# A two-layer decoder trunk: the first two weight blocks by halves of the channels, held weight splits, dummy products before the second mixer, and r·k on VectorE

## The chip, the cores and the metric

The kernel runs on one core of one Trainium2 chip. The metric is device time of one execution in microseconds (us); the time before is the median of three runs, 1817.96 us (1816.81 to 1820.01).

## The reference, cut to what matters

Two decoder layers work on 256 rows of 1024 channels, in float32:

```
h = rmsnorm(x, mix_norm_g); u = h @ w_in
y_rw  = rwkv7_time_mix(token_shift(u[rw columns]), ...)   # needs sum(r*k*r_k) per head
y_nsa = nsa_mix(u[nsa columns], ...)
x = x + concat(y_rw, y_nsa) @ w_out
x = x + cross_attention(rmsnorm(x, cross_norm_g), rmsnorm(mem, mem_norm_g), wq, wkv, wo)
x = x + (swiglu(rmsnorm(x)) in layer 0, top-2-of-8 experts in layer 1)
```

Each layer so has three places where a norm of `x` is followed by a product of all 256 rows with a large weight matrix: the mixer's input projection, the cross-attention's query projection and the channel mixer's first matrix.

## The kernel before, in words

**Three products for one.** A float32 weight block of [128 x 8 x 128] goes into two float32r parts by `split` (L382, L383): `wh`, a copy on ScalarE, and `wl = w - wh`, a subtraction on VectorE. The rows are split likewise into `hh` and `hl`. Each product of a channel group k is then three matmuls, `wh·hh`, `wh·hl` and `wl·hh` (L405 to L407), with 256 columns each. `proj_b` (L396) does this for weight blocks of 256 outputs: per block it takes one PSUM bank (tag `pj`), splits half b = 0, issues its 24 matmuls over the eight groups k, then half b = 1, and calls `evac` when both are done. The 48 matmuls of a block are one unit of work below.

**The start of a stage.** `parts_t` (L434) turns the rows: for each pair of channel groups k2 it issues four 128x128 transposes into one PSUM bank (L442), and from that bank come `hh` on ScalarE (L445) and `hl` on VectorE (L446). In the mixers, x is first scaled by the norm (`xs`, L529 to L533), so that everything waits for the sum of squares. In the cross-attention and the dense channel mixer, `norm` (L498) works on x itself and multiplies by the reciprocal norm `rb` afterwards; there the first two pairs of groups depend only on the first 512 channels of x and have high priority, and the squares (L470) are computed beside.

**Buffers.** Weight splits rotate through three buffers in the mixers, and through five (layer 0) or four (layer 1) from the cross-attention on. `pj` has two banks in a mixer, three in the cross-attention and four in the dense stage. A bank is free again when its evacuation has run: in the mixers that is `shift` (L575), a ScalarE scaling (L580) followed by a VectorE combination (L581).

**What sets the order.** Every engine runs its queue in a fixed order, drawn at build time by the framework's planner: it lists instructions by readiness, in the order of the program among those that are ready at its own reckoning of time. `behind` (L476) adds an edge that only fixes order on one engine. `hold(mark, a, v)` (L482) notes the last ScalarE and the last VectorE instruction since `mark`; of the next three weight splits, those from number a on are put behind the first of these on ScalarE, and those from number v on behind the second on VectorE. Before the change only the mixers use it (`HOLD`).

**The middle of a mixer.** `rwkv_elem` (L650) makes the elementwise quantities of the RWKV heads, woven with the NSA projections. One chain in it: `s8` is the root of a head sum (ScalarE, L689), clamped (VectorE, L692), inverted (L693), split (L640, L641), and broadcast by four matmuls (`head_bc`, L647). Beside it, GpSimd multiplies r by k (`rk`, L722), which is ready to go as soon as k has its final value (L705).

**The first mixer** also issues 20 dummy products of a matrix of ones (`WARM`, L523) while x is still on its way; the second mixer has none.

Of the kernel before, what the change touches and what calls it, by code (L numbers as in the profile page):

```python
# [10 lines left out]
ALU = mybir.AluOpType  # L11
# [26 lines left out]
HOLD = (1, 1, 2), (2, 1, 1)  # L38
XSA = (0,), (0,)
WARM = 20  # L40
TAIL = 16, 8
POOL = 2
BUSY = 2, 3, 7, 4
# [109 lines left out]
def run(gen):  # L153
    for _ in gen:
        pass
# [20 lines left out]
class Trunk:  # L176
# [216 lines left out]
    def bank3(self, tag, n):  # L393
        return self.bank(tag).rearrange("p (a b) -> p a b", a=n)

    def proj_b(self, src, hh, hl, evac, tag="pj", m=128):  # L396

        nc = self.nc
        for n in range(src.shape[0]):
            w, self.early = self.early or self.raw(src[n]), None  # L400
            ps = self.bank3(tag, 2)
            for b in range(2):
                wh, wl = self.split(w[:, b])
                for k in range(8):
                    nc.tensor.matmul(ps[:, b], wh[:, k], hh[:, k], start=(k == 0), stop=False)  # L405
                    nc.tensor.matmul(ps[:, b], wh[:, k], hl[:, k], start=False, stop=False)  # L406
                    nc.tensor.matmul(ps[:, b], wl[:, k], hh[:, k], start=False, stop=(k == 7))  # L407
                if b:
                    evac(2 * n, ps)
                yield 2.6  # L410
# [85 lines left out]
        return rb  # L496

    def norm(self, g, pool, hh, hl, junk, tag):  # L498
        with self.tc.high_priority():
            self.parts_t(self.x, g, hh, hl, tag, (0, 1))  # L500
        self.parts_t(self.x, g, hh, hl, tag, (2, 3))
        rs = self.rms(self.x, pool, junk)
        self.rb = lambda: self.bcast(rs, pool, tag, junk)[:, None, :].to_broadcast([128, 2, 256])
# [6 lines left out]
    def mixer(self, l, kvp, mc):  # L510
        nc, tc, a = self.nc, self.tc, self.a
        self.l, self.kvp = l, kvp
        self.rw = mc.enter_context(tc.tile_pool(name=f"rw{l}", bufs=1, reuse_waits="tile"))
        self.ns = mc.enter_context(tc.tile_pool(name=f"ns{l}", bufs=1, reuse_waits="tile"))
        self.psum(mc, f"pm{l}", {"rw": 3, "pj": 2, "ns": 2, "pv": 1})
        hh = self.rw.tile([128, 8, 256], F32R, name="hh")
        hl = self.rw.tile([128, 8, 256], F32R, name="hl")
        junk = self.rw.tile([128, D], F32, name="junk", tag="c9")
        if l == 0:

            ps = self.bank("pj")
            for _ in range(WARM):
                nc.tensor.matmul(ps[:, 0:128], self.one, self.one, start=True, stop=True)  # L523
        mark = len(nc.cur_bb.bb.instructions)
        rs = self.rms(self.x, self.rw, junk, both=(l == 0))
        xs = self.rw.tile([128, 2, D], F32, name="xs", tag="kb")
        for k2 in range(4):
            c = slice(256 * k2, 256 * k2 + 256)
            nc.vector.tensor_scalar(xs[:, 0, c], self.x[:, 0, c], rs[:, 0:1], None, op0=ALU.mult)  # L529
            if k2 in XSA[l]:  # L530
                nc.scalar.activation(xs[:, 1, c], self.x[:, 1, c], AF.Copy, scale=rs[:, 1:2])
            else:
                nc.vector.tensor_scalar(xs[:, 1, c], self.x[:, 1, c], rs[:, 1:2], None, op0=ALU.mult)  # L533
            self.parts_t(xs, self.vec("mix_g", l), hh, hl, "rw", (k2,))
            if k2 == HOLD[l][2]:
                self.hold(mark, *HOLD[l][:2])
        last = nc.cur_bb.bb.instructions[-1]
        run(self.proj_rwkv(hh, hl))
        if l == 0:
            mark = len(nc.cur_bb.bb.instructions)  # L540
            self.more_consts()
            for ins in nc.cur_bb.bb.instructions[mark:]:
                if ins.engine == last.engine:
                    self.behind(ins, last.name)
        self.mem_load()
        mem = self.mem_kv()
        run(weave((chain(self.rwkv_elem(), self.rwkv_chunks(), self.rwkv_out()), RC[l]),
                  (chain(self.proj_nsa(hh, hl), take(mem, M0[l]), weave((self.nsa(), 32), (mem, 42 - 2.6 * M0[l]))), 95)))

        run(self.out_proj(l))  # L550
# [33 lines left out]
    def proj_rwkv(self, hh, hl):  # L584
        nc, a, l, rw = self.nc, self.a, self.l, self.rw
        c4 = [128, 4, 256]
        self.big = rw.tile([128, 4, 4, 256], F32, name="big")
        self.r, self.k = self.big[:, 0], self.big[:, 1]
        if l == 0:
            self.v = self.vf = self.mkp.tile(c4, F32, name="vf")  # L590
        else:
            self.v = rw.tile(c4, F32, name="v", tag="kbt")
        self.wa = rw.tile([128, 256], F32, name="wa")
        self.gl = rw.tile([128, 256], F32, name="gl")
        win = a[f"win{l}"]

        def ev_w(b, ps):
            self.shift(ps[:, 0], 12, self.wa)
            self.shift(ps[:, 1], 13, self.gl)

        def ev(dst, o):
            def f(b, ps):
                for q in range(2):
                    self.shift(ps[:, q], o + b + q, dst[:, b + q])
            return f

        yield from self.proj_b(win[0:1], hh, hl, ev_w)
        yield from self.proj_b(win[1:3], hh, hl, ev(self.k, 4))
        self.tail(hh, hl)
        yield from self.proj_b(win[3:5], hh, hl, ev(self.v, 8))  # L610
        yield from self.proj_b(win[5:7], hh, hl, ev(self.r, 0))
# [38 lines left out]
    def rwkv_elem(self):  # L650
        nc, a, l, rw = self.nc, self.a, self.l, self.rw
# [4 lines left out]
        r, k, v = self.r, self.k, self.v  # L656

        mark = len(nc.cur_bb.bb.instructions)
# [60 lines left out]
            nc.gpsimd.tensor_scalar(irk[:, j], self.ind, self.vec("r_k", l)[:, j:j + 1], None, op0=ALU.mult)  # L719
        yield 10 * ELC[self.l]  # L720
        rk = rw.tile(c4, F32, name="rk", tag="c9")
        nc.gpsimd.tensor_mul(rk, r, k)  # L722
        self.b8 = self.head_parts(self.head_sum(rk, lambda j: irk[:, j]), "b8")
        if l:
            sv = self.big[:, 2]
# [432 lines left out]
    def cross(self, l, ctx):  # L1158
# [8 lines left out]
        q = cp.tile([128, 8, 256], F32, name="q", tag=tags[2])  # L1167

        def ev_q(b, ps):
            if b == 0:  # L1170
                self.rb = self.rb()
            nc.vector.scalar_tensor_tensor(q[:, b:b + 2], ps, 1.0 / 16, self.rb, op0=ALU.mult, op1=ALU.mult)

        run(self.proj_b(a[f"cq{l}"], hh, hl, ev_q))
        oh, ol = (cp.tile([128, 8, 256], F32R, name=n, tag=t) for n, t in zip(("oh", "ol"), tags))
        for h in range(4):
            ps = self.bank3("s", 2)
# [35 lines left out]
    def dense(self, ctx):  # L1213
# [11 lines left out]

        def first(s):
            got = []
            run(self.proj_b(a["dg"][s:s + 1], hh, hl, lambda b, ps: got.append(ps)))
            run(self.proj_b(a["du"][s:s + 1], hh, hl, lambda b, ps: got.append(ps)))
            return got  # L1230

        def second(s, got):
            g = gp.tile([128, 2, 256], F32, name="g")
            nc.vector.tensor_mul(g, got[0], self.rb)
            mark = len(nc.cur_bb.bb.instructions)
            nc.scalar.activation(g, g, AF.Silu)
            if s == n - 1:

                nc.scalar.activation(warm, self.eps, AF.Sqrt)
                self.chained(mark)  # L1240
            u = gp.tile([128, 2, 256], F32, name="u")
            nc.vector.tensor_mul(u, got[1], self.rb)
            nc.vector.tensor_mul(g, g, u)
            gh = gp.tile([128, 2, 256], F32R, name="gh")
            gl = gp.tile([128, 2, 256], F32R, name="gl")
            nc.scalar.copy(gh, g)
            nc.vector.tensor_sub(gl, g, gh.bitcast(F32))
            w = self.raw(a["dd"][s])
            ws = [self.split(w[:, k]) for k in range(2)]
            order = [(k, o) for k in range(2) for o in range(2)] if s < n - 1 else \  # L1250
                    [(k, o) for o in range(2) for k in range(2)]
            for k, o in order:
                wh, wl = ws[k]
                c = slice(512 * o, 512 * o + 512)
                for i in range(2):
                    t = slice(128 * i, 128 * i + 128)
                    st, sp = (s == 0 and k == 0), (s == n - 1 and k == 1)
                    nc.tensor.matmul(acc[i][o], gh[:, k, t], wh[:, c], start=st, stop=False)  # L1258
                    nc.tensor.matmul(acc[i][o], gh[:, k, t], wl[:, c], start=False, stop=False)  # L1259
                    nc.tensor.matmul(acc[i][o], gl[:, k, t], wh[:, c], start=False, stop=sp)  # L1260

        prev = None
        for s in range(n):
# [4 lines left out]
                self.rb = self.rb()  # L1268
            prev = got
        second(n - 1, prev)  # L1270
        for o in range(2):
            for i in range(2):
                xv = self.x[:, i, 512 * o:512 * o + 512]
                nc.vector.tensor_add(xv, xv, acc[i][o])
# [444 lines left out]
```

## Time and profile before

| | |
|---|---|
| median of the runs | 1817.96 us |
| the profiled execution's own time | 1818.43 us |
| its span, first to last instruction | 1816.6 us |
| mean granted TensorE clock | 0.992 |
| TensorE busy | 1772.1 us, 98% |
| VectorE, ScalarE, GpSimd busy | 1458.1, 1222.0, 68.2 us |

The profiled execution is one run with a hardware trace; "busy" is the time in which an engine has an instruction under way, the granted clock is the share of full TensorE speed (1.00 is 2.4 GHz, 0.50 is 1.2 GHz). The stages by time: first mixer 0 to 237 us, cross-attention to 305, dense channel mixer to 495, second mixer to 729, second cross-attention to 797, experts to the end.

### The profile page before, as it was taken

What the parts mean: (1) busy time and instruction counts of PE and PEld (TensorE: products, weight loads), DVE (VectorE), ACT (ScalarE), POOL (GpSimd) and SP (SyncE); (2) the same over time, 40 slices, a digit from 0 to 9 for tenths busy, and PEclk for the clock granted to TensorE, in tenths of its full rate; (3) what the DMA queues carried; (4) which work ended last, traced back from release to release, by engine and by line L of the source; (5) the groups of instructions that cost most, each with busy time, mean ns of one, the idle gap of its engine ahead of it and who ended that gap; (6) DMA issues with size and microseconds to landing.
All of it is one profiled execution on the core that took longest, in us unless ns stands there. A gap on an engine that the chain in (4) does not pass through costs nothing.

```text
span 1816.6 us, 28950 instructions
## 1 busy us (share of the span) xinstructions
PE 1772.1 (98%) x11309; PEld 1491.5 (82%) x11309; DVE 1458.1 (80%) x1947; ACT 1222.0 (67%) x1640; POOL 68.2 (4%) x152
## 2 busy tenths in 40 slices
PE   9999999999999999999999999999999999999997
PEld 8886788999898877877887888888888888888885
DVE  6777665656568766659999999999999989999997
ACT  7655455444456654558787777777777877777776
POOL 3100000000001100020001000000000000000000
PEclk9999999999999999999999999999999999999999
DMA  6442273555144422859997999998999989999990
GB/s 238 167 159 72 75 297 104 197 185 188 45 161 143 156 78 96 347 188 357 344 360 273 341 349 357 369 353 329 366 347 374 360 326 364 363 359 369 353 354 27
DMA packets 66673, 467.28 MB, mean 257 GB/s; under 512 B 7376, under 2 KB 7504, under 8 KB 11744
## 3 DMA queue, kind: packets, MB, share of 16 engines
q1 hardware_dynamic: 66208, 464.79, 69.5%
q8 instruction: 90, 1.47, 0.3%
q10 hardware_dynamic: 288, 0.52, 0.1%
q14 instruction: 55, 0.45, 0.1%
q0 software_dynamic: 32, 0.03, 0.0%
HBM read 464.27 MB, written 1.05 MB: 256 GB/s over the span
## 4 chain that ended last, share of the span: by engine, by line
PE 89%; DVE 6%; ACT 4%; issue 1%; DMA 0%; SPq 0%; ACTq 0%; DVEq 0%
PE gu L1605 11%; PE gu L1604 11%; PE gu L1603 11%; PE y L1643 6%; PE y L1642 6%; PE y L1644 6%; PE pj L405 6%; PE pj L407 6%; PE pj L406 5%; DVE wl L383 2%; PE pj L424 1%; PE pj L425 1%; PE pj L426 1%; PE tr L1619 1%; PE acc L1258 1%; PE acc L1259 1%
## 5 line engine op out<-in xcount | busy, mean ns | idle before, releaser
L383 DVE TENSOR_TENSOR wl<-raw,wh 128x1024 fp32r<-128x1024 f32 (+1 forms) x846 | 1019.8, 1219 | 195.7 <-ACT wh L382 189.3
L382 ACT CAST wh<-raw 128x1024 fp32r<-128x1024 f32 (+1 forms) x848 | 877.4, 1040 | 403.1 <-PE pj L406 135.2
L1603 PE MATMUL gu<-wh,xe 128*128 128x512 f32 x896 | 356.6, 398 | 0.0
L1605 PE MATMUL gu<-wh,xe 128*128 128x512 f32 x896 | 354.0, 395 | 0.0
L1604 PE MATMUL gu<-wl,xe 128*128 128x512 f32 x896 | 351.9, 393 | 0.0
L406 PE MATMUL pj<-hl,wh 128*128 128x256 f32 x960 | 275.2, 287 | 3.4 <-DVE hl L446 3.4
L407 PE MATMUL pj<-hh,wl 128*128 128x256 f32 x960 | 274.8, 287 | 2.0 <-DVE wl L383 2.0
L405 PE MATMUL pj<-hh,wh 128*128 128x256 f32 x960 | 275.1, 288 | 0.8 <-ACT hh L445 0.5
L1605 PEld LDWEIGHTS gu<-wh,xe 128*128 128x128 f32 x896 | 168.1, 188 | 38.5
L1604 PEld LDWEIGHTS gu<-wl,xe 128*128 128x128 f32 x896 | 168.6, 188 | 37.8
L1603 PEld LDWEIGHTS gu<-wh,xe 128*128 128x128 f32 x896 | 168.4, 188 | 35.6
L405 PEld LDWEIGHTS pj<-hh,wh 128*128 128x128 f32 x960 | 185.8, 194 | 5.9 <-issue 2.8
L406 PEld LDWEIGHTS pj<-hl,wh 128*128 128x128 f32 x960 | 185.9, 194 | 5.7 <-DVE hl L446 4.2
L407 PEld LDWEIGHTS pj<-hh,wl 128*128 128x128 f32 x960 | 186.3, 194 | 3.2 <-DVE wl L383 2.8
L1643 PE MATMUL y<-wl,hth 128*128 128x512 f32 x448 | 177.3, 396 | 2.4 <-DVE wl L383 2.4
L1642 PE MATMUL y<-wh,hth 128*128 128x512 f32 x448 | 177.7, 397 | 0.0
L1644 PE MATMUL y<-wh,htl 128*128 128x512 f32 x440 | 173.7, 395 | 0.0
L1643 PEld LDWEIGHTS y<-wl,hth 128*128 128x128 f32 x448 | 84.2, 188 | 22.5 <-DVE wl L383 2.9
L1642 PEld LDWEIGHTS y<-wh,hth 128*128 128x128 f32 x448 | 84.3, 188 | 19.7
L1644 PEld LDWEIGHTS y<-wh,htl 128*128 128x128 f32 x440 | 82.8, 188 | 19.9
L1615 DVE SCALAR_TENSOR_TENSOR h<-gu,gs,h 128x512 f32<-128x512 f32 x56 | 41.7, 745 | 1.7 <-ACT wh L382 0.9
L1078 ACT ACTIVATE pn<-pn,mx 128x128 f32<-128x128 f32 x64 | 28.5, 446 | 15.2 <-DVE mx L1075 14.8
(514 smaller groups left out, 2045.7 us busy)
## 6 DMA issues: line engine op xcount, KB each, us to landing
raw<-eg SPq DMA_DIRECT2D x106, 1024.0 KB, 5.1
raw<-eu SPq DMA_DIRECT2D x104, 1024.0 KB, 5.1
raw<-ed SPq DMA_DIRECT2D x104, 1024.0 KB, 5.2
raw<-win SPq DMA_DIRECT2D x21, 1024.0 KB, 4.9
raw<-dg SPq DMA_DIRECT2D x11, 1024.0 KB, 4.8
raw<-du SPq DMA_DIRECT2D x11, 1024.0 KB, 4.9
raw<-dd SPq DMA_DIRECT2D x11, 1024.0 KB, 4.8
raw<-ck SPq DMA_DIRECT2D x8, 1024.0 KB, 5.0
```

The lines of the kernel that those rows point to most:

```text
L382: nc.scalar.copy(wh[:, c], w[:, c])
L383: (low or nc.vector).tensor_sub(wl[:, c], w[:, c], wh[:, c].bitcast(F32))
L405: nc.tensor.matmul(ps[:, b], wh[:, k], hh[:, k], start=(k == 0), stop=False)
L406: nc.tensor.matmul(ps[:, b], wh[:, k], hl[:, k], start=False, stop=False)
L407: nc.tensor.matmul(ps[:, b], wl[:, k], hh[:, k], start=False, stop=(k == 7))
L1603: nc.tensor.matmul(ps, xe[0][:, k + kk, es], wh[:, kk], start=(k + kk == 0), stop=False)
L1604: nc.tensor.matmul(ps, xe[0][:, k + kk, es], wl[:, kk], start=False, stop=False)
L1605: nc.tensor.matmul(ps, xe[1][:, k + kk, es], wh[:, kk], start=False, stop=(k + kk == 7))
L1615: nc.vector.scalar_tensor_tensor(h, gu[1], rs, h, op0=ALU.mult, op1=ALU.mult)
L1642: nc.tensor.matmul(ys[o], hh[:, k], wh[:, c], start=st, stop=False)
L1643: nc.tensor.matmul(ys[o], hh[:, k], wl[:, c], start=False, stop=False)
L1644: nc.tensor.matmul(ys[o], hl[:, k], wh[:, c], start=False, stop=sp)
```

## The change

1. `proj_b` gets a path `one` for the first block: both halves get a PSUM bank of their own, both are split first, and the matmuls go by halves of the channels: k = 0 to 3 of output half 0, then of output half 1, then k = 4 to 7 of both. Inside a group the order becomes `wh·hh`, `wl·hh`, `wh·hl`. Each half has an evacuation of its own. It is used for the first block of both mixers, of both query projections and of the dense gate matrix.
2. `norm` calls `hold(mark, 0, 0)` behind its first two pairs: the first three weight splits of the two cross-attentions and of the dense stage go behind the row parts of channel groups 0 to 3, on ScalarE and on VectorE.
3. The second mixer begins with 14 dummy products, placed behind the dense stage's last matmul (`self.done`).
4. `rk` is computed on VectorE.

```
     def proj_b(self, src, hh, hl, evac, tag="pj", one=None):
         for n in range(src.shape[0]):
             w, self.early = self.early or self.raw(src[n]), None
+            if one and n == 0:
+                pss = [self.bank(tag)[:, 0:256] for _ in range(2)]
+                sp = [self.split(w[:, b]) for b in range(2)]
+                for ks in (range(4), range(4, 8)):
+                    for ps, (wh, wl) in zip(pss, sp):
+                        for k in ks:
+                            nc.tensor.matmul(ps, wh[:, k], hh[:, k], start=(k == 0), stop=False)
+                            nc.tensor.matmul(ps, wl[:, k], hh[:, k], start=False, stop=False)
+                            nc.tensor.matmul(ps, wh[:, k], hl[:, k], start=False, stop=(k == 7))
+                for b in range(2):
+                    one(b, pss[b])
+                yield 5.2
+                continue
...
     def norm(self, g, pool, hh, hl, junk, tag):
+        mark = len(self.nc.cur_bb.bb.instructions)
         with self.tc.high_priority():
             self.parts_t(self.x, g, hh, hl, tag, (0, 1))
+        self.hold(mark, 0, 0)
         self.parts_t(self.x, g, hh, hl, tag, (2, 3))
...
+        else:
+            ps = self.bank("pj")
+            for _ in range(KEEP):
+                self.behind(nc.tensor.matmul(ps[:, 0:128], self.one, self.one, start=True, stop=True).ins, self.done)
...
-            self.shift(ps[:, 0], 12, self.wa)
-            self.shift(ps[:, 1], 13, self.gl)
+        def one_w(b, ps):
+            self.shift(ps, 12 + b, (self.wa, self.gl)[b])
...
-        nc.gpsimd.tensor_mul(rk, r, k)
+        nc.vector.tensor_mul(rk, r, k)
...
+        def one_q(b, ps):
             if b == 0:
                 self.rb = self.rb()
+            nc.vector.scalar_tensor_tensor(q[:, b], ps, 1.0 / 16, self.rb[:, b], op0=ALU.mult, op1=ALU.mult)
...
         def second(s, got):
-            nc.vector.tensor_mul(g, got[0], self.rb)
+            for b, ps in enumerate(got[:-1]) if s == 0 else ():
+                nc.vector.tensor_mul(g[:, b], ps, self.rb[:, b])
+            if s:
+                nc.vector.tensor_mul(g, got[0], self.rb)
```

`KEEP` is 14, and `self.done` is the name of the dense stage's last instruction.

## Rows read from the trace of the kernel before

**Rows 1.** The page: busy time, and the chain that ended last, by engine.

```profile
PE 1772.1 (98%) x11309; PEld 1491.5 (82%) x11309; DVE 1458.1 (80%) x1947; ACT 1222.0 (67%) x1640; POOL 68.2 (4%) x152
...
PE 89%; DVE 6%; ACT 4%; issue 1%; DMA 0%; SPq 0%; ACTq 0%; DVEq 0%
```

**Rows 2.** Waits of TensorE, whole span: us in total, times, longest.

```profile
PE rw L647 <- DVE r L641: 8.5, 2, 4.2
```

**Rows 3.** Busy us by stretch (PE, PEld, DVE, ACT, POOL; records), PEclk, DMA, GB/s.

```profile
79.00:83.20 4.20, 0.00 (x0) 0.00 (x1) 4.17 (x5) 1.35 (x2) 0.00 (x0) 0.99 0.00 0
83.20:86.60 3.40, 3.40 (x16) 3.40 (x17) 2.40 (x3) 0.17 (x1) 0.00 (x0) 0.51 0.81 279
86.60:90.00 3.40, 3.40 (x30) 3.40 (x30) 2.49 (x3) 1.49 (x2) 0.00 (x0) 1.00 0.24 53
...
573.60:578.00 4.40, 4.40 (x20) 4.40 (x21) 2.50 (x4) 1.04 (x1) 0.00 (x0) 0.50 0.70 238
```

**Rows 4.** VectorE, timeline of 55 to 100 us: start, us, operation.

```profile
76.10 2.54 DVE L692 TENSOR_SCALAR s<-s 128x256 f32<-128x256 f32 x1
...
79.93 1.75 DVE L693 RECIPROCAL s<-s 128x256 f32<-128x256 f32 x1
...
87.51 1.23 DVE L383 TENSOR_TENSOR wl<-raw,wh 128x1024 fp32r<-128x1024 f32 x1 [1.88 <-ACT wh L382]
```

**Rows 5.** GpSimd, timelines of both layers.

```profile
73.95 4.55 POOL L722 TENSOR_TENSOR rk<-big 128x1024 f32<-128x1024 f32 x1 [8.44 <-DVE big L705]
...
589.11 2.47 POOL L734 TENSOR_TENSOR dv<-vf,v 128x1024 f32<-128x1024 f32 x1 [0.40 <-PE rw L632]
```

**Rows 6.** VectorE at the second mixer's start: a 128x256 scaling.

```profile
498.48 0.35 DVE L533 TENSOR_SCALAR xs<-x,rs 128x256 f32<-128x256 f32 x1
```

**Rows 7.** Busy us by stretch at the five stage starts, columns as in rows 3.

```profile
7.80:13.50 5.70, 3.99 (x28) 3.32 (x29) 5.40 (x14) 4.75 (x11) 4.91 (x27) 1.00 0.98 401
13.50:19.10 5.60, 5.14 (x39) 4.63 (x39) 5.57 (x16) 2.40 (x3) 3.72 (x16) 1.00 0.69 239
237.30:240.20 2.90, 1.22 (x7) 0.70 (x6) 2.90 (x6) 2.57 (x6) 0.00 (x0) 0.99 0.76 220
240.20:243.40 3.20, 3.19 (x15) 3.19 (x16) 2.59 (x5) 2.63 (x6) 0.00 (x0) 0.50 1.04 438
243.40:247.65 4.25, 4.25 (x37) 4.25 (x37) 3.21 (x9) 3.33 (x7) 0.00 (x0) 0.98 1.00 418
304.50:307.30 2.80, 1.94 (x18) 1.75 (x17) 2.44 (x4) 2.10 (x5) 0.00 (x0) 1.00 0.74 217
307.30:313.80 6.50, 6.25 (x50) 5.91 (x49) 4.00 (x12) 6.43 (x15) 0.00 (x0) 1.00 0.17 71
498.40:506.20 7.80, 7.50 (x37) 6.93 (x38) 6.04 (x15) 4.28 (x10) 0.00 (x0) 0.57 0.28 108
506.20:510.00 3.80, 3.64 (x30) 3.44 (x30) 3.48 (x5) 1.19 (x2) 0.00 (x0) 0.98 0.00 0
731.70:735.20 3.50, 3.41 (x16) 3.41 (x17) 2.89 (x6) 2.80 (x6) 0.00 (x0) 0.52 1.01 424
```

**Rows 8.** TensorE, timelines: first mixer's dummies, second mixer's and dense stage's transposes.

```profile
1.07 6.41 PE L523 MATMUL pj<-one 128*128 128x128 f32 x40 [1.07 <-POOL sh L579]
...
498.45 1.77 PE L442 MATMUL rw<-ident,xs 128*128 128x128 f32 x12 [2.87 <-DVE xs L529]
...
305.55 1.97 PE L442 MATMUL acc<-ident,x 128*128 128x128 f32 x16 [0.86 <-DVE x L1208]
```

**Rows 9.** ScalarE and VectorE at the cross-attention's and the dense stage's start.

```profile
234.74 1.05 ACT L382 CAST wh<-raw 128x1024 fp32r<-128x1024 f32 x1 [2.58 <-PE ns L567]
...
235.69 0.83 ACT L445 ACTIVATE hh<-tr,cross_g 128x256 fp32r<-128x256 f32 x2
...
303.07 1.23 DVE L383 TENSOR_TENSOR wl<-raw,wh 128x1024 fp32r<-128x1024 f32 x1 [1.57 <-ACT wh L382]
```

**Rows 10.** VectorE in the first mixer: the first evacuation.

```profile
22.50 0.47 DVE L581 SCALAR_TENSOR_TENSOR wa<-pj,omm,sh 128x256 f32<-128x256 f32 x1
```

More of the change, by code (lines that the diff above doesn't have):

```diff
@@ L40 @@
 WARM = 20
+KEEP = 14
 TAIL = 16, 8
@@ L394, in bank3, with proj_b @@
         return self.bank(tag).rearrange("p (a b) -> p a b", a=n)
-    def proj_b(self, src, hh, hl, evac, tag="pj", m=128):
+    def proj_b(self, src, hh, hl, evac, tag="pj", one=None):
         nc = self.nc
@@ L595, in proj_rwkv @@
         win = a[f"win{l}"]
-        def ev_w(b, ps):
-            self.shift(ps[:, 0], 12, self.wa)
-            self.shift(ps[:, 1], 13, self.gl)
+        def one_w(b, ps):
+            self.shift(ps, 12 + b, (self.wa, self.gl)[b])
         def ev(dst, o):
@@ L605, in ev @@
             return f
-        yield from self.proj_b(win[0:1], hh, hl, ev_w)
+        yield from self.proj_b(win[0:1], hh, hl, None, one=one_w)
         yield from self.proj_b(win[1:3], hh, hl, ev(self.k, 4))
@@ L1169, in ev_q @@
         def ev_q(b, ps):
+            nc.vector.scalar_tensor_tensor(q[:, b:b + 2], ps, 1.0 / 16, self.rb, op0=ALU.mult, op1=ALU.mult)
+        def one_q(b, ps):
             if b == 0:
                 self.rb = self.rb()
-            nc.vector.scalar_tensor_tensor(q[:, b:b + 2], ps, 1.0 / 16, self.rb, op0=ALU.mult, op1=ALU.mult)
-        run(self.proj_b(a[f"cq{l}"], hh, hl, ev_q))
+            nc.vector.scalar_tensor_tensor(q[:, b], ps, 1.0 / 16, self.rb[:, b], op0=ALU.mult, op1=ALU.mult)
+        run(self.proj_b(a[f"cq{l}"], hh, hl, ev_q, one=one_q))
         oh, ol = (cp.tile([128, 8, 256], F32R, name=n, tag=t) for n, t in zip(("oh", "ol"), tags))
@@ L1227, in first @@
             got = []
-            run(self.proj_b(a["dg"][s:s + 1], hh, hl, lambda b, ps: got.append(ps)))
+            run(self.proj_b(a["dg"][s:s + 1], hh, hl, lambda b, ps: got.append(ps),
+                            one=None if s else lambda b, ps: got.append(ps)))
             run(self.proj_b(a["du"][s:s + 1], hh, hl, lambda b, ps: got.append(ps)))
@@ L1241, in second @@
             u = gp.tile([128, 2, 256], F32, name="u")
-            nc.vector.tensor_mul(u, got[1], self.rb)
+            nc.vector.tensor_mul(u, got[-1], self.rb)
             nc.vector.tensor_mul(g, g, u)
@@ L1270, in dense @@
         second(n - 1, prev)
+        self.done = nc.cur_bb.bb.instructions[-1].name
         for o in range(2):
```

## The prediction

> **What bounds the kernel now.** The page comes first. TensorE is busy for 98% of the span and makes up 89% of the chain that ended last [rows 1]: only what fills a hole in TensorE's queue, or lets it run at full clock, moves the end. The waits of TensorE by who ended them come next. They are few, and the largest is the broadcast L647 waiting for `r`, 8.5 us in two waits [rows 2]. The stretches show what such a hole costs beyond itself: TensorE does nothing from 79.0 to 83.2, then the granted clock is 0.51 and 16 matmuls take 3.4 us where the next 3.4 us hold 30, so about 0.11 to 0.12 us each at full clock [rows 3]. The same stretches around the stage starts show the rest: at 240.2, 498.4 and 731.7 the clock is near 0.5 as well, always behind a stretch in which TensorE had waited [rows 7, 8]. The experts, more than half of the time, aren't touched, so the sum is one of a few us out of 1818. A measurement of this kernel tells about 0.2%, 3.6 us, from no change.
>
> **r·k on VectorE.** GpSimd's `rk` runs from 73.95 for 4.55 us, to 78.50; the clamp of `s` on VectorE starts at 76.10 and lasts 2.54, to 78.64 [rows 4, 5]. A scaling of the same 128x256 takes 0.35 [rows 6], and GpSimd's other multiplication-like pass of this size takes 2.47 [rows 5]: the clamp stands until GpSimd lets go. It lies on the chain to `r`, whose end TensorE awaits. So the clamp shortens by 2.54 - 0.35 = 2.2 us per layer, 4.4 in both. On VectorE `rk` costs 1.23, by the subtraction of the same 128x1024 [rows 4]. Where it lands in the queue I take from its rank: it stands behind clamp, inverse, split and the weight subtractions already due, and VectorE has a hole of 1.88 us before 87.51 [rows 4], which hides it; if that cover is gone, it delays `r` by 1.23 per layer. What is late next is `r` still, by 4.2 - 2.2 = 2.0 us. With the wait halved I count half of the slow clock gone: at 83.2 it costs 3.4 - 16 x 0.12 = 1.5, in the second layer 4.4 - 20 x 0.12 = 2.0 [rows 3], together 3.5, half 1.7. Term: **-6.1**; ends -7.9 (all of the slow clock gone) and +2.5 (no gain, `rk` on the chain twice).
>
> **Second mixer.** TensorE idles 2.87 us to 498.45 [rows 8]; from 498.4 to 510.0 it issues 67 matmuls and transposes in 11.6 us, most of it at clock 0.57 [rows 7], which at 0.12 would be 8.0: 3.6 are lost. The dummies are two instructions each (20 are 40 records [rows 8]), so 28; at 1.97 / 16 = 0.12 us [rows 8] they take 3.4 us and end about 498.8, 0.4 behind the time at which the transposes can go. VectorE, busy 6.04 of the first 7.8 us [rows 7], then sets the pace, and halves let TensorE work on channel groups 0 to 3 for both output halves meanwhile. I take **-3.0**; ends -3.6 and +2.9, the latter if the dummies run at half speed, 28 x 0.21 = 5.9 us, to 501.3.
>
> **Cross-attentions.** From 237.30 to 247.65, 59 instructions take 10.35 us instead of 7.1: 3.3 lost, part in waits for `hl` and `wl`, part at clock 0.50 [rows 7]. The cause is an order: on ScalarE the second cast of the new weights stands before the first row parts and waits 2.58 us for a buffer of the output projection, so `hh` starts at 235.69 though its transposes are long done [rows 9]. `hold` turns that round. Behind the held casts on ScalarE stand the squares and the row parts 4 to 7, and behind the held subtractions on VectorE the additions to x; the first half's 24 matmuls per output pair, 24 x 0.12 = 2.9 us, cover most of that. The second cross-attention repeats the pattern, with 16 instructions in 3.5 us at 0.52 [rows 7]. I take 2.2 each, **-4.4**; ends -6.6 and, if the held splits are late, +8.6 (last rival). Splitting the evacuation in two and moving `rb` forward costs nothing here, as three banks leave a whole block, 48 x 0.12 = 5.8 us, before one is needed again.
>
> **First mixer.** From 7.8 to 19.1, 67 instructions take 11.3 us instead of 8.0 [rows 7]; but the early part of the loss, before the first `hl`, is left as it is, since `HOLD` stays. I take **-0.6**; ends -1.2 and +2.5. The latter end is the banks: both now go to the first block, so the second waits for the first evacuation. `wa` came at 22.50 to 22.97 [rows 10], 3.9 us behind the block's end at 19.1; the first half now ends 12 x 0.12 = 1.4 earlier, which leaves 2.5 if the queues keep their order. I expect less, since with `wh·hl` last the bank and the weight buffer come free together, and the evacuation ranks ahead of the next cast.
>
> **Dense stage.** Only 1.1 us are lost from 304.5 to 313.8 (68 instructions, 8.2 at 0.12) [rows 7]. Here x is complete only at the stage's start, and all 16 transposes run in a row from 305.55 [rows 8]; the splits that `hold` now delays were made before, under the output product, the one at 303.07 for instance [rows 9]. They lose that cover: a cast of 1.05 and a subtraction of 1.23 [rows 9] come behind the row parts, 2.3 us, of which the two halves win back some. Term: **+1.5**; ends -1.0 and +7.1.
>
> **Sum.** -6.1 - 3.0 - 4.4 - 0.6 + 1.5 = -12.6 against the profiled execution's 1818.43, so 1805.8; the median of the runs is 0.5 lower, 1805.4. I say 1805.5. The favourable ends add up to -20.3, or 1797.7.
>
> **Rivals.** *The clock falls all the same.* Behind the dummies come transposes and then matmuls at the pace of VectorE, and behind the shorter wait for `r` still 2 us of nothing. Against: from 7.8 to 13.5 TensorE was busy 3.99 of 5.7 us, transposes among it, and the clock stayed at 1.00 [rows 7]. For: it fell at 240.2 behind a stretch with 1.22 of 2.9 busy [rows 7]. Then the 1.7 of the slow clock behind `r` stay, and as much in the second mixer: -12.6 + 3.4 = -9.2, 1808.7. Chance 0.20.
>
> The Trainium skill, TensorE: Matmul & The Clock Gate, Part 4: PE-mode transpose, says that transposes do not count as a busy TensorE in the way matmuls do; by that rule the transposes behind the dummies would help the clock to fall, and the time would be this rival's. The stretch from 7.8 to 13.5 in rows 7 does not bear it out, as far as dummies that had just run do not hide it.
>
> *The held splits only pay at the mixers.* The cross-attentions gain nothing, as the casts now come where the wait was, and the dense stage loses 3.6. -6.1 - 3.0 - 0.6 + 3.6 = -6.1, 1811.9. For it: the dense rows; against: ScalarE idles 2.58 us before 234.74 [rows 9]. Chance 0.12.
>
> *The change does not do what it says for r.* `rk` lands ahead of `r`, or the clamp was slow for another cause: -12.6 + 6.1 + 2.5 = -4.0, 1814.0. Chance 0.08.
>
> *Slower: casts behind everything that ranks ahead of them.* In the three norm stages the squares and all eight row parts come before the weights in program order. If the casts start only behind these, in the dense stage 8 x 0.42 + 4 x 0.82 = 6.6 us (hh by half of the pair in rows 9, a square with its read as long as two of them) lie between the first transpose and the first cast; the two splits and the rest of the block then end 7.1 later than now, and by the same count each cross-attention 4.3. +15.7 with the first half of `r` (-4.4) and the second mixer (-3.0) kept gives +8.3, 1826.3. It decides from a loss of 7.4 in the three starts on. Against: in the cross-attentions the second half of x comes too late to be ranked ahead. Chance 0.05.
>
> **Numbers.** Forecast 0.55, with its own range of 1800 to 1811; the rivals 0.20, 0.12, 0.08 and 0.05. Faster by over 0.2% (below 1814.3): the forecast, the first two rivals and half of the third, less a little for their own spread, 0.87; slower, the last, 0.05; the same 0.08. The range for 8 in 10 is 1798 to 1815: from the favourable ends to just past the third rival.
>
> **What would show it.** Right: the clamp L692 at about 0.35 us; the wait of L647 at about 2 us in both layers; PEclk near 1.00 over the first 10 us of the second mixer; `hh` of groups 0 to 3 ahead of the first cast in the cross-attentions; the first 48 matmuls of each start nearer to 6 us. Wrong: `rk` standing between the inverse and `r`; casts in the dense stage later than 310; TensorE waiting for `wa` at the second block of a mixer; a total gain under 4 us with these signs present, which would mean that the time is given back later in the woven part of the mixers.

## The result and the profile after

The changed kernel takes 1829.41 us (median, 1828.43 to 1830.58), the kernel before on the same chip 1818.88: ratio 1.0059, interval 1.0042 to 1.0077. That is 10.5 us slower, where 12.5 us faster was forecast. The profiled span went from 1816.6 to 1827.2.

The page, busy time and chain [rows 1]: TensorE works 8 us more, with 28 more records (the dummies), and still makes up the chain.

```profile
PE 1779.7 (97%) x11337; PEld 1498.1 (82%) x11337; DVE 1457.1 (80%) x1952; ACT 1221.0 (67%) x1640; POOL 57.6 (3%) x150
...
PE 90%; DVE 5%; ACT 3%; issue 1%; DMA 1%; SPq 0%; ACTq 0%; DVEq 0%
```

Waits of TensorE over the span (total, times, longest). The wait for `r`, 8.5 us before [rows 2], is 4.0. New beside it are the waits for `hl` at the transposes (4.6), for a cast of the weights (3.8) and for `xb` (2.5). The others stand in the kernel before too: 2.4 us for `wl` at `y`, 2.0 for `wl` and 3.4 for `hl` at the products of `proj_b`.

```profile
PE tr L457 <- DVE hl L461: 4.6, 2, 2.3
PE rw L668 <- DVE r L662: 4.0, 2, 2.0
PE pj L409 <- ACT wh L383: 3.8, 2, 3.6
PE pj L410 <- DVE wl L384: 2.6, 4, 0.9
PE ns L1016 <- POOL xb L1007: 2.5, 1, 2.5
PE y L1672 <- DVE wl L384: 2.4, 1, 2.4
...
PE pj L411 <- DVE hl L461: 1.5, 1, 1.5
```

Where the time went, by stage. A stage ends where VectorE's last addition to x ends in its timeline; a length is the difference of two such ends, the experts run to the end of the span.

| stage | before | changed | difference |
|---|---|---|---|
| first mixer | 238.24 | 235.45 | -2.8 |
| first cross-attention | 67.25 | 69.04 | +1.8 |
| dense | 190.81 | 195.99 | +5.2 |
| second mixer | 233.39 | 235.94 | +2.5 |
| second cross-attention | 68.29 | 70.59 | +2.3 |
| experts | 1018.62 | 1020.19 | +1.6 |

**Dense start.** ScalarE's timeline: seven row parts (`hh`) and two squares come first, the first cast of the weights only at 307.98, the second at 310.94. In the kernel before these two began at 301.99 and 304.77 and the first subtraction at 303.07 [rows 9], under the output product and ahead of the end of the last addition to x (305.49).

```profile
304.24 0.47 ACT L460 ACTIVATE hh<-acc,ffn_g 128x256 fp32r<-128x256 f32 x1 [9.79 <-PE acc L457]
304.61 0.62 ACT L485 ACTIVATE junk<-x 128x512 f32<-128x512 f32 x1
...
305.23 1.92 ACT L460 ACTIVATE hh<-acc,ffn_g 128x256 fp32r<-128x256 f32 x5
307.01 0.66 ACT L485 ACTIVATE junk<-x 128x512 f32<-128x512 f32 x1
...
307.62 0.50 ACT L460 ACTIVATE hh<-acc,ffn_g 128x256 fp32r<-128x256 f32 x1
307.98 1.08 ACT L383 CAST wh<-raw 128x1024 fp32r<-128x1024 f32 x1
...
310.94 3.88 ACT L383 CAST wh<-raw 128x1024 fp32r<-128x1024 f32 x4
```

TensorE's timeline of the same stretch: 16 transposes, 3.57 us of nothing, then products whose rows last 0.41 us instead of 0.28. The busy time by stretch (columns as in rows 3) has the clock: 0.50 over 6.7 us, where before it stayed at 1.00 [rows 7].

```profile
303.61 1.93 PE L457 MATMUL acc<-ident,x 128*128 128x128 f32 x16
309.11 0.58 PE L409 MATMUL pj<-hh,wh 128*128 128x256 f32 x1 [3.57 <-ACT wh L383]
310.37 0.58 PE L410 MATMUL pj<-hh,wl 128*128 128x256 f32 x1 [0.68 <-DVE wl L384]
310.74 0.41 PE L411 MATMUL pj<-hl,wh 128*128 128x256 f32 x1
```

```profile
304.50:308.00 3.50, 1.03 (x10) 0.76 (x8) 2.70 (x7) 3.50 (x12) 0.00 (x0) 0.99 0.00 0
308.00:314.70 6.70, 4.92 (x21) 4.62 (x22) 5.45 (x9) 6.67 (x9) 0.00 (x0) 0.50 0.13 23
```

**First cross-attention.** Two `hh` are made at 229.77, but VectorE's queue has the two additions to x ahead of the first `hl`; `hl` comes at 235.36, ScalarE's next `hh` waits 4.66 us for it, and the first, held cast comes at 237.25, 1.8 us behind the end of the last addition (235.45). In the kernel before even the second cast, at 234.74 [rows 9], came 3.5 us ahead of that end (238.24). First ScalarE's timeline, then VectorE's:

```profile
235.88 0.86 ACT L460 ACTIVATE hh<-tr,cross_g 128x256 fp32r<-128x256 f32 x2 [4.66 <-DVE hl L461]
...
237.25 1.03 ACT L383 CAST wh<-raw 128x1024 fp32r<-128x1024 f32 x1
```

```profile
234.76 0.69 DVE L595 TENSOR_TENSOR x<-x,ns 128x512 f32<-128x512 f32 x1 [0.71 <-PE ns L589]
235.36 1.89 DVE L461 SCALAR_TENSOR_TENSOR hl<-tr,cross_g,hh 128x256 fp32r<-128x256 f32 x4
```

**r.** VectorE's timeline: the clamp takes 0.28 us instead of 2.54 [rows 4], and `rk` stands behind `r`.

```profile
74.40 0.28 DVE L713 TENSOR_SCALAR s<-s 128x256 f32<-128x256 f32 x1
...
78.71 0.47 DVE L662 SCALAR_TENSOR_TENSOR r<-h,low,s 128x256 fp32r<-128x256 f32 x1
79.10 1.22 DVE L743 TENSOR_TENSOR rk<-big 128x1024 f32<-128x1024 f32 x1
```

**Second mixer, behind r.** GpSimd's timeline: its three passes for `v` now run at 583 to 596, before the memset of `xb`. VectorE's timeline below it: three subtractions take 5.71 us and three additions of 128x120 to `xb` 3.92; one alone takes 1.22 and 0.34. TensorE waits 2.5 us for `xb` and then has 3.4 us at clock 0.51.

```profile
583.43 2.74 POOL L755 TENSOR_TENSOR dv<-vf,v 128x1024 f32<-128x1024 f32 x1 [1.82 <-PE rw L653]
591.08 2.37 POOL L756 TENSOR_TENSOR dv<-dv,big 128x1024 f32<-128x1024 f32 x1 [4.91 <-ACT big L753]
593.52 2.48 POOL L757 TENSOR_TENSOR vf<-v,dv 128x1024 f32<-128x1024 f32 x1
595.95 0.12 POOL L1007 MEMSET xb<- 128x32 f32 x1
```

```profile
582.68 5.71 DVE L384 TENSOR_TENSOR wl<-raw,wh 128x1024 fp32r<-128x1024 f32 x3
...
592.24 3.92 DVE L1012 TENSOR_TENSOR xb<-vc,vecs 128x120 f32<-128x120 f32 x3 [0.42 <-PE ns L1016]
...
596.86 0.34 DVE L1012 TENSOR_TENSOR xb<-vc,vecs 128x120 f32<-128x120 f32 x1
```

In the kernel before, the memset came ahead of the passes, the first of which is in rows 5, and GpSimd stood idle for 12.65 and 5.69 us on the way there:

```profile
581.53 1.36 POOL L784 TENSOR_SCALAR_AFFINE_SELECT sub<-one 128x256 f32<-128x256 f32 x1 [12.65 <-DVE ar L709]
588.58 0.13 POOL L986 MEMSET xb<- 128x32 f32 x1 [5.69 <-PE ns L995]
```

In both kernels the first pass waits for TensorE's head sum of `rk`, the matmuls that add up r·k per head (0.40 us in rows 5, 1.82 above): the pass writes to the buffer that `rk` had. In TensorE's order that head sum moved forward, from 588.13 in the kernel before (first row) to 582.60 (second row), though this stage begins 4.2 us later.

```profile
588.13 0.38 PE L632 MATMUL rw<-rk,irk 128*32 128x256 f32 x1
582.60 0.64 PE L653 MATMUL rw<-rk,irk 128*32 128x256 f32 x8
```

### The profile page after: what moved, and what is told of

Same layout as the page of the kernel before. It is cut to its first block, busy times and chain, and to the rows that moved or that the text cites. A ratio compares the mean times of both kernels' runs of the same rounds, so it can differ in the third digit from the quotient of the medians.

```text
span 1827.2 us, 29007 instructions
## 1 busy us (share of the span) xinstructions
PE 1779.7 (97%) x11337; PEld 1498.1 (82%) x11337; DVE 1457.1 (80%) x1952; ACT 1221.0 (67%) x1640; POOL 57.6 (3%) x150
## 4 chain that ended last, share of the span: by engine, by line
PE 90%; DVE 5%; ACT 3%; issue 1%; DMA 1%; SPq 0%; ACTq 0%; DVEq 0%
PE gu L1634 11%; PE gu L1633 11%; PE gu L1632 11%; PE y L1672 6%; PE y L1671 6%; PE y L1673 6%; PE pj L420 5%; PE pj L422 5%; PE pj L421 5%; PE pj L439 2%; PE pj L440 1%; DVE wl L384 1%; PE pj L441 1%; PE tr L1648 1%; PE acc L1286 1%; PE acc L1287 1%
## 5 line engine op out<-in xcount | busy, mean ns | idle before, releaser
L420 PE MATMUL pj<-hh,wh 128*128 128x256 f32 x880 | 251.6, 286 | 0.1
L422 PE MATMUL pj<-hh,wl 128*128 128x256 f32 x880 | 251.1, 285 | 0.0
L421 PE MATMUL pj<-hl,wh 128*128 128x256 f32 x880 | 250.1, 284 | 0.0
L420 PEld LDWEIGHTS pj<-hh,wh 128*128 128x128 f32 x880 | 169.3, 192 | 3.6 <-issue 2.2
L422 PEld LDWEIGHTS pj<-hh,wl 128*128 128x128 f32 x880 | 169.3, 192 | 1.8 <-issue 1.2
L421 PEld LDWEIGHTS pj<-hl,wh 128*128 128x128 f32 x880 | 169.3, 192 | 1.1 <-issue 0.7
```

## The experiments

Each kernel was timed against the kernel before on the same chip. A result gives the median in us, its difference from the median of the kernel before, and the ratio with its 95% interval. Such an interval reaches 1.5 to 2.5 us to either side, so a difference of under some 3 us between two experiments is carried by the rows named with it and not by the medians alone. Line numbers in rows are those of the kernel named.

**1. The changed kernel without the hold.**

```
         with self.tc.high_priority():
             self.parts_t(self.x, g, hh, hl, tag, (0, 1))
-        self.hold(mark, 0, 0)
```

> The changed kernel without the hold in the three norm stages (first casts and subtractions free again to run ahead of the row parts). Placement theory: the changed kernel loses 5.1 us at the dense start and 1.6 to 2.3 at each cross-attention because the held splits lost the output product that covered them; without the hold some 9 us come back, and against the kernel before the time is +1 to +2 us (about 1.001). Rival, the halves cost it (two banks for one block, evacuation in two pieces): the loss stays, +8 to +10 us (1.005).

1816.52 us against 1818.06, -1.5; ratio 0.9986 (0.9977 to 0.9995). The hold alone turned the sign: against the changed kernel's +10.5 it is worth some 12 us, more than the 9 expected. The rival falls.

**2. r·k on VectorE alone.**

```
-        nc.gpsimd.tensor_mul(rk, r, k)
+        nc.vector.tensor_mul(rk, r, k)
```

> The kernel before with r k on VectorE and nothing else. Queue theory: the clamp shortens by 2.2 us per layer and the second mixer keeps its clock, but GpSimd, free earlier, then does the three passes for v ahead of the small memset that the compression awaits, and gives back 3 to 4 us in the second mixer; the sum is -1 to -3 us. Rival, the give-back comes from another part of the change (the shifted start of the mixer): -5 to -7 us, with no TensorE wait for the memset.

1820.39, +2.3; 1.0010 (1.0001 to 1.0020). The clamp took 0.28 us and the wait for `r` 4.1 in two, the first mixer became 2.4 us shorter (235.82 us), the second 4.5 longer (237.92), with the same 2.5 us wait for `xb`. The rival falls, since no other part of the change is in this kernel; more was given back than the queue theory expected. Its "GpSimd, free earlier" is not what the rows show: the head sum that lets the passes go comes at 578.75 instead of 588.13, while `rk` itself is done no earlier (570.0 us on VectorE, 568.9 on GpSimd in the kernel before).

**3. The hold alone**, on the kernel before.

```
+        mark = len(self.nc.cur_bb.bb.instructions)
         with self.tc.high_priority():
             self.parts_t(self.x, g, hh, hl, tag, (0, 1))
+        self.hold(mark, 0, 0)
```

> The kernel before with the hold in the three norm stages and nothing else. Placement theory: +8 to +11 us, of which about 5 at the dense start (first cast behind the squares and the row parts) and 2 at each cross-attention. Rival, the hold only hurts together with the halves: 0 to -4 us.

1830.47, +12.4; 1.0069 (1.0055 to 1.0083), a little over the +8 to +11 of the placement theory; the rival falls. TensorE's waits from 230 to 330 us are those of the changed kernel:

```profile
PE pj L405 <- ACT wh L382: 3.8, 2, 3.6
PE tr L442 <- DVE hl L446: 2.3, 1, 2.3
```

**4. The dummies alone.**

```
+        else:
+            ps = self.bank("pj")
+            for _ in range(KEEP):
+                self.behind(nc.tensor.matmul(ps[:, 0:128], self.one, self.one, start=True, stop=True).ins, self.done)
```

> The kernel before with the dummy products ahead of the second mixer and nothing else. Clock theory: the granted clock stays at 1.00 over the first 10 us of the second mixer and the start is 2 to 3.6 us shorter. Rival, VectorE sets the pace there (the scaling of mem stands ahead of the first row part): the clock stays up, but TensorE waits for row parts instead and the gain is under 1.5 us. Second rival, the transposes queue behind the dummies: 0 to +1 us.

1819.03, +1.0; 1.0003 (0.9994 to 1.0012): no gain. The clock theory falls; the first rival is right about the wait for row parts and wrong about the clock. The clock was at 1.00 to 503.0 and then fell all the same, behind a new wait of 1.7 us for `hl` (columns as in rows 3):

```profile
496.20:503.00 6.80, 4.72 (x39) 4.15 (x38) 4.76 (x15) 4.29 (x12) 0.00 (x0) 1.00 0.45 155
503.00:506.40 3.40, 3.40 (x17) 3.40 (x18) 3.40 (x6) 1.80 (x4) 0.00 (x0) 0.51 0.21 58
```

**5. The halves alone**: the path `one` and its evacuations, no hold, no dummies, `rk` on GpSimd.

> The kernel before with the first two blocks by halves alone (no hold, no dummies, r k on GpSimd as before). Theory: the halves are what gained in the run without the hold (about 2 us at each cross-attention, 0.9 at the dense start, 1 at the first mixer), so -5 to -6 us against the kernel before. Rival, they gained only together with the other parts: 0 to -2 us.

1810.97, -6.7; 0.9959 (0.9945 to 0.9972). The rival falls: the halves, which the prediction hardly priced by themselves, are the gain. How long each start takes, from the end of the last addition to x to the start of the 145th product (the first three blocks issued), read from the timelines, in us:

| kernel | first cross | dense | second mixer | second cross |
|---|---|---|---|---|
| before | 21.41 | 20.25 | 28.03 | 21.45 |
| changed | 23.27 | 25.42 | 26.83 | 23.79 |
| hold alone | 23.90 | 26.38 | 27.73 | 23.08 |
| halves alone | 19.31 | 19.31 | 25.71 | 19.38 |
| dummies alone | 21.51 | 20.24 | 28.41 | 21.52 |
| halves and dummies (10) | 19.32 | 19.31 | 28.26 | 19.39 |
| the same, scaling of `mem` behind (8) | 19.32 | 19.25 | 25.32 | 19.38 |
| halves, later splits held (11) | 20.28 | 20.74 | 25.72 | 20.09 |

**6. The scaling of `mem` behind the row parts**, without the hold.

```
-            nc.vector.tensor_scalar(vm[:, i], vm[:, i], self.mrs[:, i:i + 1], None, op0=ALU.mult)
+            ins = nc.vector.tensor_scalar(vm[:, i], vm[:, i], self.mrs[:, i:i + 1], None, op0=ALU.mult).ins
+            if l:
+                self.behind(ins, self.last)
```

`self.last` is the name of the last `hl` instruction.

> The changed kernel without the hold, and in the second mixer the scaling of mem on VectorE put behind the last row part. Theory: TensorE's 1.3 to 1.5 us wait for the first hl goes, so 1 to 1.5 us less than without this edit: -3.5 to -4 us against the kernel before. Rival, VectorE has as much to do in that stretch either way: no less than without the edit, -2.5 us, and the wait only moves.

1813.15, -4.5; 0.9974 (0.9964 to 0.9985): 3.0 below run 1. The start took 25.31 us instead of 26.65, 1.3 of it, as the theory has it; the rest of the 3.0 is not accounted for. In the profiled executions 2.2 us of the difference lie in the experts, where the clock fell for 3.4 us in run 1 and not in run 6.

**7. The memset of `xb` on VectorE**, without the hold.

```
-            nc.gpsimd.memset(xb[:, :, 30:32], 0.0)
+            nc.vector.memset(xb[:, :, 30:32], 0.0)
```

> The changed kernel without the hold, and the compression's memset on VectorE instead of GpSimd. Theory: TensorE's 2.5 us wait for xb behind GpSimd's three passes goes, and 1.7 of slow clock with it, so 3 to 4 us less than without this edit: -5.5 to -6.5 us against the kernel before. Rival, what is given back in the woven part is the order of the work and not that wait: under 1 us less, -2.5 to -3.5 us, with a wait of the same size elsewhere.

1812.93, -4.7; 0.9973 (0.9962 to 0.9983): 3.2 below run 1, but the theory's step fell: TensorE still waited 2.3 us at 588, now for the additions. Their rows told why. One addition begins 0.64 us after GpSimd's last pass for `v` has begun and ends 0.14 us after that pass has ended: 2.00 us for what takes 0.34 a moment later. First VectorE, then GpSimd:

```profile
584.95 2.00 DVE L1011 TENSOR_TENSOR xb<-vc,vecs 128x120 f32<-128x120 f32 x1
...
587.26 0.34 DVE L1011 TENSOR_TENSOR xb<-vc,vecs 128x120 f32<-128x120 f32 x1
```

```profile
584.31 2.50 POOL L756 TENSOR_TENSOR vf<-v,dv 128x1024 f32<-128x1024 f32 x1
```

So it is not only the memset's place in the queue: it is the passes too.

**8. r·k back on GpSimd**, the rest as in run 6.

> The changed kernel without the hold and with r k back on GpSimd; the scaling of mem behind the last row part as in the run before. Theory: r k on VectorE costs some 2 us net as long as the memset waits, so this is 2 us below that run: -5.5 to -6.5 us against the kernel before. Rival, r k on VectorE is worth its price once the rest stands: this is 2 us above that run, -1.5 us.

1811.01, -6.7; 0.9962 (0.9949 to 0.9976), 2.1 below run 6: as expected. All five executions lie below all eight of run 6, on the same chip.

**9. Halves, with r·k and the three passes for `v` on VectorE.**

```
-            nc.gpsimd.tensor_sub(d, self.vf, v)
-            nc.gpsimd.tensor_mul(d, d, sv)
-            nc.gpsimd.tensor_add(self.vf, v, d)
+            nc.vector.tensor_sub(d, self.vf, v)
+            nc.vector.tensor_mul(d, d, sv)
+            nc.vector.tensor_add(self.vf, v, d)
```

> The kernel before with the halves, r k on VectorE, and the three passes for v (dv, dv, vf) on VectorE too, so that GpSimd holds nothing up; no hold, no dummies. Collision theory: what r k on VectorE gives back in the second mixer (some 6 us) is GpSimd's three passes, come forward, that stop VectorE's additions to xb or delay the memset; with them gone both gains for r stay: -9 to -12 us against the kernel before. Rival, it is the order in which the woven work then stands: -4.5 to -6 us, no better than the halves alone.

1809.90, -8.1; 0.9949 (0.9936 to 0.9963): better than the rival, short of the theory by 1 us.

**10. Halves and dummies**, without run 6's edit.

> The kernel before with the halves and the dummies, without the edit that puts the scaling of mem behind the row parts. Theory: the halves alone already kept the clock in the second mixer, and the dummies add nothing but bring the scaling of mem ahead of the first hl, so this is 1 to 1.5 us above the halves alone: -5 to -5.7 us. Rival, the dummies are free or help: -6.7 us or less.

1814.19, -3.9; 0.9974 (0.9963 to 0.9985): 2.8 above the halves alone, so worse than expected; in the table the start is 2.6 us longer. VectorE's timeline shows the scaling of `mem`, which needs a DMA, ahead of the first `hl`:

```profile
495.72 0.75 DVE L1165 TENSOR_SCALAR vm<-vm,mrs 128x1024 f32<-128x1024 f32 x1 [0.86 <-DMA vm<-mem]
496.39 2.04 DVE L461 SCALAR_TENSOR_TENSOR hl<-rw,vecs,hh 128x256 fp32r<-128x256 f32 x5
```

In the halves alone the row parts come first (495.71) and both scalings at 501.79. So the dummies moved the planner's order on another engine.

**11. A hold for the second and third split only**, with the halves.

```
+        self.hold(mark, 1, 1)
```

> The kernel before with the halves and a hold that leaves the first split free and holds only the second and third behind the row parts of groups 0 to 3. Cover theory: the first split stays under the output product, only the cast that waited for a buffer ahead of the first row part goes behind it: 0 to 2 us less at each cross-attention, 0 to +1 at the dense start, -7 to -10 us in all. Rival, any split behind row parts is late: 1 to 3 us more at each start, 0 to -3 us in all.

1815.74, -2.3; 0.9987 (0.9978 to 0.9996): 4.4 above the halves without it. Each of the three starts with a hold is 0.7 to 1.4 us longer in the table, 3.1 in all; the other 1.3 was not traced. The cover theory in this form falls: at these starts a later split behind the row parts is late too.

**12. Halves and r·k on VectorE, the passes left on GpSimd**: the partner of run 9.

> The kernel before with the halves and r k on VectorE, the three passes for v left on GpSimd: the partner of the run that had them on VectorE (-8.1 us). Collision theory: the passes come forward on GpSimd and hold the compression up, so the second mixer is 3.5 to 5 us longer than in the partner and the time -3 to -5 us against the kernel before, with a TensorE wait for xb of some 2.5 us near 590. Rival, the passes are innocent: within 1 us of the partner, -7 to -9 us.

1815.92, -2.7; 0.9985 (0.9976 to 0.9994): 5.5 above run 9 by the differences. The collision theory's -3 to -5 is just missed, the rival falls. The start of the second mixer took the same in both (26.96 and 27.00 us), the whole second mixer 236.81 and 230.52. The partner's waits in that mixer, and the additions to `xb` by line, in this kernel and in run 9 (min/median/max in ns):

```profile
PE ns L1009 <- POOL xb L1000: 2.6, 1, 2.6
...
PE ns L1009 <- DVE xb L1005: 0.5, 1, 0.5
```

```profile
L1005 DVE TENSOR_TENSOR xb<-vc,vecs x8: 339/347/2382, 95.7 to 589.4; 128x120 f32<-128x120 f32 x8
```

```profile
L1005 DVE TENSOR_TENSOR xb<-vc,vecs x8: 351/360/371, 95.5 to 586.9; 128x120 f32<-128x120 f32 x8
```

With the passes off GpSimd no addition stands (371 ns at most instead of 2382), and TensorE has no wait for `xb`. Of the 6.3 us between the two mixers 3.1 are these waits; two stretches at clock 0.50 (from 566.0 and 589.9), which run 9 does not have, make up some 3 more, at 1.5 each by the working of rows 3, and run 9 has a wait of 1.1 for `hl` of its own. The other 1.3 was not traced. The first of these stretches, behind the wait for `r` that both kernels have, begins ten us ahead of the first pass (576.67), so it is not the passes' doing. Counted in TensorE's instructions done, run 12's lead over the kernel before falls by 7.3 us between 585 and 650 us of that kernel, run 9's by 2.5: that puts 4.8 us down to where the passes run.

**13. The best parts together**: run 6 with the passes for `v` on VectorE.

> The best parts together: halves, dummies with the scaling of mem behind the last row part, r k and the three passes for v on VectorE, no hold. Theory: the second mixer's start is 1.7 us shorter than in the run without dummies (25.3 us from the last addition to x to the 145th product, as with r k on GpSimd, instead of 27.0), so -9 to -10 us against the kernel before. Rival, the start is won and given back in the woven part: -7 to -8 us.

1808.99, -9.6; 0.9949 (0.9936 to 0.9963). The gain is the one expected. The medians of runs 9 and 13 lie too close to rank them, but both beat both kernels. The profiled execution, 1805.72, is the fastest of the five. VectorE's timeline and the stretch at the second mixer's start: row parts first, scaling last, clock 1.00.

```profile
493.35 2.44 DVE L461 SCALAR_TENSOR_TENSOR hl<-rw,vecs,hh 128x256 fp32r<-128x256 f32 x6
...
498.76 1.41 DVE L1166 TENSOR_SCALAR vm<-vm,mrs 128x1024 f32<-128x1024 f32 x2
```

```profile
488.00:501.00 13.00, 12.65 (x98) 11.66 (x98) 10.85 (x24) 8.74 (x19) 0.10 (x1) 1.00 0.32 103
```

## Why the prediction was wrong, point by point

By the parts alone the sign is the hold's: +12.4 for the hold, +2.3 for r·k, +1.0 for the dummies and -6.7 for the halves add up to +9.0, where +10.5 was measured together.

**The rival with 0.05 came true.** "Slower: casts behind everything that ranks ahead of them" gave 1826.3; 1829.4 was measured. Its dense step is the row at 307.98: seven of the eight row parts and two of the four squares stand ahead of the first cast. It priced the dense stage at +7.1 and each cross-attention at +4.3; they cost +5.2, +1.8 and +2.3 with the halves in place, and less the halves' own gain that is +6.1, +4.0 and +4.4 (the changed kernel against the halves alone in the table). That its sum came so near is in part luck: it kept -4.4 for `r` and -3.0 for the second mixer, where run 2 gave +2.3 and run 4 +1.0, and it took nothing off for the halves, which gave -6.7 (run 5).

**The cross-attention term, -4.4, was +4.1: the step that failed** is "the first half's 24 matmuls ... cover most of that". The cast's wait ahead of `hh` was there, but the splits that the hold delays had been made under the output projection's last products. Held, they begin when those products are over, and there is nothing left for the first half to cover them with. The argument against the rival, that the second half of x comes too late to be ranked ahead, was beside the point: what came ahead on VectorE were the additions to x, at 234.76, and the first `hl` behind them. The gain lay in the halves: alone they took 2.1 us off each of these starts.

**The dense term, +1.5, was mis-sized**: +5.2. The loss of cover was named, and priced as one split of 2.3 us. It was TensorE waits of 3.57 and 0.68 us and, behind them, 6.7 us at clock 0.50, in which 21 records at 0.21 instead of 0.12 us each (rows 3 give both) cost 21 x 0.09 = 1.9: some 6.2 in all, near the 6.1 of the line above. The slow clock was not counted at all.

**The r·k term, -6.1, had its mechanism right and its sum wrong.** Clamp 0.28 us, wait 2.0 in both layers, and one of the two slow stretches behind `r` gone: all as named, though in runs 2 and 12 the second layer's clock fell behind that wait all the same (at 569.0 and 566.0). The first mixer gained from it. The step that failed is "what is late next is `r` still", as the end of the account: `r` was late by the 2.0 named, but `xb` came late behind it. `rk` was followed as a load on one engine and a relief of the other, not to what waits for its result. In the planner's new order TensorE's head sum of `rk` came forward, from 588.13 to 582.60, and with it GpSimd's passes for `v`, ahead of the memset; GpSimd had stood idle before them in the kernel before too, so the 4.55 us that it was freed of did not let them go earlier. They stopped VectorE again, where TensorE waited for it. That very effect, a VectorE instruction that stands until GpSimd lets go, was the reason given for the gain. Runs 2 and 12 show the give-back, run 9 takes most of it away: counted as in run 12, the lead falls behind `r` by 7.3 us in runs 2 and 12 and by 2.5 in runs 9 and 13. Why the planner moved the head sum is not shown.

**The second mixer's term, -3.0, was -1.2 at the start.** The dummies ran at full speed (28 records in 3.29 us from 499.59, the clock at 1.00), and the end of +2.9 did not come. What failed is the order: they were costed on TensorE alone. In the planner's order they brought the scaling of `mem` from behind the row parts to ahead of the first `hl`, 1.5 us of TensorE's wait in the changed kernel. With that undone (runs 6, 8 and 13) the start takes 25.3 us, 2.7 less than before, close to the term. (The end of the dummies was put 0.2 us early: by rows 8 TensorE's wait begins at 498.45 - 2.87 = 495.58, not 495.4. Nothing hangs on it.) Of the 2.7 the halves alone give 2.3 when the clock holds; in runs 9 and 12 it did not, and they needed 27.0.

**The first mixer's term, -0.6, is too small where the clock holds.** The 145th product starts at 32.24 us instead of 33.94, -1.7, and at 32.35 with the halves alone. But in runs 1, 8, 9 and 12, which have the halves there too, it comes at 33.56 to 34.16: there the clock was 0.50 for 3.4 us from 12.2 to 13.0 us on. The halves are not the cause: run 2, which has the start of the kernel before, has that slow stretch too (34.31). Of the stage's -2.8 the shorter wait for `r`, 2.2 us, leaves 1.1; where the other 1.1 is given back was not traced.

**The experts' +1.6 is likely not the change's.** The wait of 2.4 us for `wl` stands in both kernels; behind it the clock fell in this execution (first row of TensorE's timeline, then the stretch), and in that of the halves alone too, but not in that of the kernel before. Of the fifteen kernels' profiles nine have this slow stretch; the cause of the difference is open.

```profile
1000.69 0.69 PE L1672 MATMUL y<-wl,hth 128*128 128x512 f32 x1 [2.43 <-DVE wl L384]
```

```profile
1000.80:1004.30 3.50, 3.50 (x9) 2.73 (x10) 3.50 (x4) 1.04 (x1) 0.00 (x0) 0.51 0.38 110
```

**What the signs said.** Four of the five signs for "right" came: the clamp, the wait for `r`, the clock in the second mixer, and `hh` ahead of the first cast. The fifth, a start nearer to 6 us for 48 products, came half way and misled. From the first product to the 49th it took 8.5 us instead of 10.4 in the first cross-attention, but the 49th came 11.4 us behind the end of x instead of 9.5; in the dense stage the first of these is 8.9 instead of 6.6. Of the signs for "wrong", the first dense cast at 307.98 stayed short of the 310 named, the second, at 310.94, did not; and that time is given back later in the woven part of the mixers is what run 2 shows.

**Open:** some 2 us that the second mixer still gives back behind `r` in run 13 (its lead over the kernel before, counted in TensorE's instructions done, goes from 13.4 us at 585 to 10.9 at 624), and 1.3 us between runs 9 and 12.

## What to carry to other kernels

A hold that puts work behind something fixes one wait by giving up whatever covered that work: ask first what the held instruction runs under today, and what it will run under then. When work moves between two engines, follow also what waits for its result: here a sum of `rk` and three passes on the engine that `rk` had left came earlier, and collided in a new place. Where a planner draws the order, an addition on one engine can reorder another: read every queue around it, not the one that was edited.

## What the runs showed of the hardware

A VectorE instruction can stand until a GpSimd pass ends, and not only one with a single input like the clamp: an addition of 128x120 took 2.00 us instead of 0.34 (run 7), and three subtractions of 128x1024 took 5.71 instead of 3.66 (the changed kernel). The Trainium skill, SBUF — State Buffer, section "SBUF: two separate sides", says that VectorE and GpSimd share one pair of ports, that whichever starts first holds it for its whole instruction, and that a VectorE instruction with two inputs in SBUF counts among those that are shut out while GpSimd reads. The traces agree: the addition of run 7 ends 0.14 us behind the GpSimd pass in whose time it began, and with the passes moved to VectorE the longest addition is 371 ns.

The clock fell behind the same wait in one profile and not in another: behind the experts' 2.4 us, behind 0.9 us for `wl` in the first mixer (at 12.2 us in run 8, not in the halves alone), and at the second mixer's start with the halves, which took 25.7 or 27.0 us. Executions of the kernel before itself spread in experiments 9 to 11 from 1815.13 us, at a mean clock of 0.995, to 1820.97 at 0.989. So a term under 2 us that hangs on the clock may be won in a share of the executions only.
